# Eight Strassen-like pairs of the second product beside the last column tiles of gate and up

## The chip, the cores and the metric

The kernel runs on one core of a Trainium2 chip. Engines: TensorE (PE, with its weight load PEld), VectorE (DVE), ScalarE (ACT), GpSimd (POOL) and SyncE (SP, here only the queue that issues transfers). PSUM, which PE writes, is used as eight banks of one tile each (128 partitions x 512 float32). Times are device microseconds; the metric is the median of several runs.

## The reference, cut to what matters

```
# DEPTH = 2, SEQ = 256, D_MODEL = 1024, D_FF = 2816
def swiglu(x, w_in, w_out):
    h = x @ w_in
    gate, up = h[..., :D_FF], h[..., D_FF:]
    return (jax.nn.silu(gate) * up) @ w_out
...
for l in range(DEPTH):
    x = layer_norm(ALPHA * x + 0.5 * swiglu(x, ffn1_w_in[l], ffn1_w_out[l]), ln_g[l, 0], ln_b[l, 0])
    mix = hybrid_mixer(x, ...)        # two kinds of attention, one input and one output projection
    x = layer_norm(ALPHA * x + mix, ln_g[l, 1], ln_b[l, 1])
    x = layer_norm(ALPHA * x + 0.5 * swiglu(x, ffn2_w_in[l], ffn2_w_out[l]), ln_g[l, 2], ln_b[l, 2])
```

Four feed-forwards run, named here by layer and place: 00, 02, 10 and 12 (the last). The change is in them alone; the mixer stays as it is.

## The kernel before

All float32 products are made of parts: a value is split into a high part (`wh`, a cast on ACT) and the rest (`wl`, a subtraction on DVE), and three matmuls (high x high, high x rest, rest x high) take the place of one. Weights come through the class `Weights`: a transfer on SP into one of five `raw` buffers of 128 x 1024, then `wh` on ACT and `wl` on DVE, each into one of nine buffers. `get(i)` has the next weights prepared as far as `LOOK` + 1 = 9 slots go. These splits have lower priority (`high_priority(-LATER)`) in the order that a scheduler makes for DVE, ACT and SP. On PE the order is that of the code (`manual_schedule`).

A feed-forward has four stages:

- `first`: the first four column tiles of gate and up as one product of 1024 columns.
- 18 column tiles j = 4 to 21 by `col`, mostly in pairs. Each has a gate half `hg` and an up half `hu`; a half is 8 matmuls of 512 columns (`wide`, both token tiles with high and rest of x) and 8 of 256 columns (`narrow`), in one PSUM bank. Two tiles use four banks, and the next two the other four. The *gather* of a half is an ACT copy of the bank's second part and a DVE add (`L434`, `L435`); after it the bank is free. Then ACT makes silu, DVE the product, and `g` is split for the second product.
- The second product, `w_out`: 22 row tiles of 128 rows. A row tile k is either ordinary (`step`: 12 matmuls of 512 columns for both token tiles t) or half of a pair q (rows 2q, 2q+1) that is multiplied by a Strassen-like scheme (`pair`): 7 products of 3 matmuls, 21 in place of 24, on sums of g (`sums`, four DVE operations, a cast and a subtraction) and on sums of weights (`_make_pair`: two transfers `raw..a`, `raw..b`, a third raw buffer `raw..t` for sums, four DVE sums, and splits named `b`, `t`, `a` of 1024 and `f` of 512 columns). Before, `STR` names six pairs, and `PLAN` sets them among three ordinary tiles, after all column tiles. Accumulators are four banks `acc` (token tile, half of the columns) and four `pp` (products 5, 7, 1, 6).
- The tail: `TAIL` = 7 ordinary row tiles for token tile 0, the layer norm of token tile 0, the same row tiles for token tile 1, and between them (`TCUT` = 3 steps before the end) the transposes `tr_y` of the normalized tile 0.

What waits for what is set by semaphores: a matmul that starts a new tile in a bank waits for the last reader of the old one, a transfer into a raw buffer for its last reader, a split for its transfer.

Of the kernel before, what the change touches and what calls it, by code (L numbers as in the profile page):

```python
# [33 lines left out]
TAIL = 7  # L34
SPLIT = 3
TCUT = 3
LOOK = 8
# [3 lines left out]
STR = (3, 4, 5, 6, 7, 8)  # L41
PLAN = "o o S o S S S S S"
# [17 lines left out]
class Weights:  # L60
# [6 lines left out]
    def _halves(self, i, raw, nm=""):  # L67
        nc = self.nc
        n = raw.shape[-1]
        wh = self.pool.tile([P, 1024], F32R, tag="wh", name=f"wh{i}{nm}", bufs=9)  # L70
        wl = self.pool.tile([P, 1024], F32R, tag="wl", name=f"wl{i}{nm}", bufs=9)
        nc.scalar.copy(wh[:, 0:n], raw)
        nc.vector.tensor_tensor(wl[:, 0:n], raw, wh[:, 0:n].bitcast(F32), ALU.subtract)
        return [tuple(w[:, c : c + 512] for w in (wh, wl)) for c in range(0, n, 512)]
# [21 lines left out]
    def _slots(self, i):  # L96
        return 4 if self.srcs[i][0] == "S" else 1

    def _make(self, i):
# [4 lines left out]
        wh = self.pool.tile([P, 1024], F32R, tag="wh", name=f"wh{i}", bufs=9)  # L104
        wl = self.pool.tile([P, 1024], F32R, tag="wl", name=f"wl{i}", bufs=9)
# [30 lines left out]
def encoder_kernel(  # L136
# [36 lines left out]

    singles = [k for k in range(JT) if k // 2 not in STR]
    singles, tail = singles[: len(singles) - TAIL], singles[len(singles) - TAIL :]
    plan, left, pairs = [], list(singles), list(STR)
    for u in PLAN.split():
        plan.append((u, (left if u == "o" else pairs).pop(0)))
    assert not left and not pairs

    def out_rows(w):
        row = lambda k: w[k * P : (k + 1) * P, :]
        rows = [row(k) if u == "o" else ("S", row(2 * k), row(2 * k + 1)) for u, k in plan]
        return rows + [row(k) for k in tail]

    srcs = []
    for l in range(DEPTH):
        srcs += [f1_b[l, k] for k in range(KT)]
        srcs += [f1_in[l, j, s] for j in range(JT - NB) for s in range(2)]
        srcs += out_rows(f1_out[l])  # L190
# [8 lines left out]
        srcs += [f2_b[l, k] for k in range(KT)]  # L199
        srcs += [f2_in[l, j, s] for j in range(JT - NB) for s in range(2)]  # L200
        srcs += out_rows(f2_out[l])
# [159 lines left out]
    def ffn(l, n, last=False):  # L361
        nonlocal wi
        nm = f"{l}{n}"
        gs = [gp.tile([P, 2, 2, SEQ], F32R, tag="g", name=f"g_{nm}_{q}") for q in range(JT // 2)]
# [29 lines left out]
        def first_t(gv, t):  # L394
# [3 lines left out]
            for q in range(2):  # L398
                a = slice(t * P, (t + 1) * P)
                dh = gs[q][:, :, 0, a]  # L400
                nc.scalar.copy(dh, tr[:, 2 * q : 2 * q + 2, :])
                dv.tensor_tensor(gs[q][:, :, 1, a], tr[:, 2 * q : 2 * q + 2, :], dh.bitcast(F32), ALU.subtract)

        def col(*js, flip=False):
# [3 lines left out]
            for j in js:  # L408

                hs = [ps.tile([P, 2, SEQ], F32, tag="b", name=f"h{'gu'[s]}_{nm}_{j}") for s in range(2)]  # L410
                tl = tp.tile([P, 2, SEQ], F32, tag="tl", name=f"tl_{nm}_{j}", bufs=2)
                ws = [W.get(wi), W.get(wi + 1)]
                wi += 2
                ts.append((j, hs, tl, ws))

            def wide(hs, ws, s):
                for k in range(KT):

                    mm(hs[s], ws[s][0][:, k * P : (k + 1) * P], xx[:, k], start=(k == 0 and not flip),  # L419
                       stop=(k == KT - 1 and flip), skip_group_check=flip)  # L420

            def narrow(hs, ws, s):
                for k in range(KT):
                    mm(hs[s][:, 1, :], ws[s][1][:, k * P : (k + 1) * P], xx[:, k, 0], start=(k == 0 and flip),  # L424
                       stop=(k == KT - 1 and not flip), skip_group_check=flip)

            one, two = (narrow, wide) if flip else (wide, narrow)
            for j, hs, tl, ws in ts:
                for s in range(2):
                    one(hs, ws, s)  # L430
            for j, hs, tl, ws in ts:
                for s in range(2):
                    two(hs, ws, s)
                    nc.scalar.copy(tl[:, s], hs[s][:, 1, :])  # L434
                    dv.tensor_tensor(tl[:, s], hs[s][:, 0, :], tl[:, s], ALU.add)  # L435
                nc.scalar.activation(tl[:, 0], tl[:, 0], AF.Silu)  # L436
                gv = tl[:, 1]
                dv.tensor_tensor(gv, tl[:, 0], gv, ALU.mult)  # L438
                q, jj = divmod(j, 2)
                n = P if q in STR and jj == 0 else SEQ  # L440
                nc.scalar.copy(gs[q][:, jj, 0, 0:n], gv[:, 0:n])  # L441
                dv.tensor_tensor(gs[q][:, jj, 1, 0:n], gv[:, 0:n], gs[q][:, jj, 0, 0:n].bitcast(F32), ALU.subtract)
                if q in STR and jj:
                    sums(q, ts[0][2][:, 1], gv)

        sm = {}

        def sums(q, g0, g1):

            f = tp.tile([P, 4, P], F32, tag="tmp", name=f"sf_{nm}_{q}")  # L450
            if STR.index(q) < 3:
                s = xp.tile([P, 2, 4, P], F32R, tag="x", name=f"s_{nm}_{q}")
                sh, sl = s[:, 0], s[:, 1]
            else:
                sh, sl = (tp.tile([P, 4, P], F32R, tag="tmp", name=f"s{c}_{nm}_{q}") for c in "hl")
# [22 lines left out]
        for j in (NB + 1, *range(NB + 2, JT, 2)):  # L478

            col(*((j,) if j == NB + 1 else (j, j + 1)), flip=(j % 4 == 0 or j == NB + 1))  # L480
# [3 lines left out]
            if j == JT - 6:  # L484
                gb = load_gb(l, n)
                if n == 0:
                    load_mix(l)

        k0, k1 = singles[0], tail[-1]
        kl = tail[-SPLIT]  # L490
        acc = [[(slice(512 * h, 512 * h + 512), ps.tile([P, 512], F32, tag="b", name=f"acc_{nm}_{t}{h}"),
                 k0, tail[-SPLIT - 1] if last and t and h else k1) for h in range(2)] for t in range(2)]
# [12 lines left out]
        pp = {}  # L505

        def pair(q, w, first, final):
            b11, b21, b22, t4, t1, t2, t3 = w
            if first:
                for c in (5, 7, 1, 6):  # L510
                    pp[c] = ps.tile([P, 512], F32, tag="b", name=f"pp_{nm}_{c}")
            sh, sl = sm[q]
            blk = lambda kk, t: [gs[q][:, kk, e, t * P : (t + 1) * P] for e in range(2)]
            smb = lambda c: (sh[:, c], sl[:, c])
            s1, s2, s3, s4 = (smb(c) for c in range(4))
            for o, (ah, al), (bh, bl) in (
                (acc[0][0][1], blk(1, 0), b21),
                (acc[0][1][1], s4, b22),
                (pp[5], s1, t1),
                (pp[7], s3, t3),  # L520
                (pp[1], blk(0, 0), b11),
                (pp[6], s2, t2),
                (acc[1][0][1], blk(1, 1), t4),
            ):
                own = any(o is p for p in pp.values())
                for e, (g, ww) in enumerate(((ah, bh), (ah, bl), (al, bh))):
                    mm(o, g, ww, start=(own and first and e == 0), stop=(own and final and e == 2))  # L527

        for u, k in plan:
            w = W.get(wi)  # L530
            wi += 1
            if u == "S":
                pair(k, w, k == STR[0], k == STR[-1])
# [448 lines left out]
```

## Time and profile before

| | |
|---|---|
| median of three runs | 930.16 us (928.87 to 930.35) |
| the profiled execution: own time, span | 929.28 us, 927.5 us |
| mean granted TensorE clock | 0.997 |
| busy: PE, DVE, ACT | 919.1 us (99%), 804.9 us (87%), 577.8 us (62%) |
| `wl` splits on DVE (L119) | 325.2 us in 271 |
| `wh` casts on ACT (L118) | 282.1 us in 271 |
| transfer of 512 KB, issue to landing | 4.4 to 4.5 us (median) |
| chain that ended last | PE 98% |

A row of a profile's timeline gives start, length, engine, line, operation, the tile written and those read, shapes and count, and in brackets the idle time of the engine before it and what ended it. Lengths overlap: an engine starts its next instruction before the last one has ended. The interval from start to start is what an instruction costs in a row of them.

### The profile page before, as it was taken

What the parts mean: (1) busy time and instruction counts of PE and PEld (TensorE: products, weight loads), DVE (VectorE), ACT (ScalarE), POOL (GpSimd) and SP (SyncE); (2) the same over time, 40 slices, a digit from 0 to 9 for tenths busy, and PEclk for the clock granted to TensorE, in tenths of its full rate; (3) what the DMA queues carried; (4) which work ended last, traced back from release to release, by engine and by line L of the source; (5) the groups of instructions that cost most, each with busy time, mean ns of one, the idle gap of its engine ahead of it and who ended that gap; (6) DMA issues with size and microseconds to landing.
All of it is one profiled execution on the core that took longest, in us unless ns stands there. A gap on an engine that the chain in (4) does not pass through costs nothing.

```text
span 927.5 us, 13795 instructions
## 1 busy us (share of the span) xinstructions
PE 919.1 (99%) x4958; PEld 784.9 (85%) x4958; DVE 804.9 (87%) x1388; ACT 577.8 (62%) x982; POOL 17.0 (2%) x27
## 2 busy tenths in 40 slices
PE   9999999999999999999999999999999999999996
PEld 6888888888878888888888888888888888888885
DVE  7898899998987677899986888999988876888997
ACT  5768656546865666656646666664478656666660
POOL 0000000000000000000000000000000000000000
PEclk9999999999999999999999999999999999999998
DMA  8976445774426755545775665466844365665451
GB/s 320 313 265 203 160 137 191 246 260 154 128 90 206 248 182 182 159 136 191 257 262 196 187 192 168 136 231 208 290 112 137 100 236 188 189 192 163 136 205 46
DMA packets 51380, 176.30 MB, mean 190 GB/s; under 512 B 6512, under 2 KB 8304, under 8 KB 51312
## 3 DMA queue, kind: packets, MB, share of 16 engines
q1 hardware_dynamic: 51024, 175.03, 58.0%
q8 instruction: 39, 0.64, 0.3%
q10 hardware_dynamic: 288, 0.39, 0.1%
q14 instruction: 29, 0.24, 0.1%
HBM read 174.35 MB, written 1.05 MB: 189 GB/s over the span
## 4 chain that ended last, share of the span: by engine, by line
PE 98%; DMA 1%; DVE 1%; SPq 0%; issue 0%; ACT 0%; DVEq 0%
PE hg L419 14%; PE hu L419 14%; PE acc L503 12%; PE hb L381 9%; PE hu L424 7%; PE hg L424 7%; PE pp L527 7%; PE acc L527 5%; PE ao L840 5%; PE os L776 1%; PE pj_sq L617 1%; PE pj_sq L619 1%; PE pj_dv L617 1%; PE pj_sq L618 1%; PE pj_dq L618 1%; PE pj_dv L619 1%
## 5 line engine op out<-in xcount | busy, mean ns | idle before, releaser
L119 DVE TENSOR_TENSOR wl<-raw,wh 128x1024 fp32r<-128x1024 f32 (+1 forms) x271 | 325.2, 1207 | 57.0 <-PE hg L424 20.2
L118 ACT CAST wh<-raw 128x1024 fp32r<-128x1024 f32 (+1 forms) x271 | 282.1, 1046 | 99.7 <-PE acc L503 14.8
L419 PE MATMUL hg<-xx,wh 128*128 128x512 f32 x576 | 143.1, 390 | 0.0
L419 PE MATMUL hu<-xx,wh 128*128 128x512 f32 x576 | 142.3, 389 | 0.0
L419 PEld LDWEIGHTS hu<-xx,wh 128*128 128x128 f32 x576 | 108.1, 188 | 22.5
L419 PEld LDWEIGHTS hg<-xx,wh 128*128 128x128 f32 x576 | 106.6, 188 | 21.2
L503 PE MATMUL acc<-wh,g 128*128 128x512 f32 (+1 forms) x326 | 90.5, 386 | 0.0
L424 PE MATMUL hg<-xx,wl 128*128 128x256 f32 x576 | 81.0, 283 | 0.0
L424 PE MATMUL hu<-xx,wl 128*128 128x256 f32 x576 | 80.9, 283 | 0.0
L424 PEld LDWEIGHTS hg<-xx,wl 128*128 128x128 f32 x576 | 75.4, 191 | 1.6
L424 PEld LDWEIGHTS hu<-xx,wl 128*128 128x128 f32 x576 | 74.3, 192 | 0.0
L503 PEld LDWEIGHTS acc<-wh,g 128*128 128x128 f32 x326 | 60.9, 188 | 12.2
L381 PE MATMUL hb<-wh,xx 128*128 128x512 f32 x256 | 69.5, 391 | 0.4 <-ACT wh L118 0.4
L381 PEld LDWEIGHTS hb<-wh,xx 128*128 128x128 f32 x256 | 47.7, 188 | 11.3 <-ACT wh L118 1.6
L503 PE MATMUL acc<-wl,g 128*128 128x512 f32 (+1 forms) x163 | 51.7, 385 | 0.0
L434 ACT COPY tl<-hg 128x256 f32<-128x256 f32 x72 | 26.7, 371 | 30.9 <-PE hg L419 27.4
L434 ACT COPY tl<-hu 128x256 f32<-128x256 f32 x72 | 26.9, 373 | 19.6 <-PE hu L424 16.8
L381 PE MATMUL hb<-wl,xx 128*128 128x512 f32 x128 | 38.9, 390 | 0.0
L441 ACT CAST g<-tl 128x128 fp32r<-128x128 f32 (+1 forms) x72 | 26.7, 371 | 19.2 <-DVE tl L438 18.2
L840 PE MATMUL ao<-wh,xx 128*128 128x512 f32 x128 | 37.0, 398 | 0.0
L503 PEld LDWEIGHTS acc<-wl,g 128*128 128x128 f32 x163 | 30.6, 188 | 6.1
L436 ACT ACTIVATE tl<-tl 128x256 f32<-128x256 f32 x72 | 30.1, 418 | 6.5 <-DVE tl L435 5.7
(1140 smaller groups left out, 1576.3 us busy)
## 6 DMA issues: line engine op xcount, KB each, us to landing
raw<-in_f_in_dram SPq DMA_DIRECT2D x144, 512.0 KB, 4.4
raw<-in_f_out_dram SPq DMA_DIRECT2D x40, 512.0 KB, 4.5
raw<-in_m_in_dram SPq DMA_DIRECT2D x36, 512.0 KB, 4.4
raw<-in_f_b_dram SPq DMA_DIRECT2D x29, 512.0 KB, 4.3
raw<-in_m_out_dram SPq DMA_DIRECT2D x8, 512.0 KB, 5.0
raw<-in_m_out_dram SPq DMA_DIRECT2D x16, 256.0 KB, 4.4
lng<-in_ln_g_dram SPq DMA_DIRECT2D x6, 512.0 KB, 4.9
lnb<-in_ln_b_dram SPq DMA_DIRECT2D x6, 512.0 KB, 6.2
```

The lines of the kernel that those rows point to most:

```text
L118: nc.scalar.copy(wh[:, s], raw[:, s])
L119: nc.vector.tensor_tensor(wl[:, s], raw[:, s], wh[:, s].bitcast(F32), ALU.subtract)
L381: mm(hb[s], xx[:, k, g, t, :], ww[:, 512 * s : 512 * s + 512], start=(k == 0 and e == 0), stop=(k == KT - 1 and e == 2))
L419: mm(hs[s], ws[s][0][:, k * P : (k + 1) * P], xx[:, k], start=(k == 0 and not flip), stop=(k == KT - 1 and flip), skip_group_check=flip)
L424: mm(hs[s][:, 1, :], ws[s][1][:, k * P : (k + 1) * P], xx[:, k, 0], start=(k == 0 and flip), stop=(k == KT - 1 and not flip), skip_group_c ...
L434: nc.scalar.copy(tl[:, s], hs[s][:, 1, :])
L436: nc.scalar.activation(tl[:, 0], tl[:, 0], AF.Silu)
L441: nc.scalar.copy(gs[q][:, jj, 0, 0:n], gv[:, 0:n])
L503: mm(a, g, ww[:, s], start=(k == ka and e == 0), stop=(k == kb and e == 2))
L527: mm(o, g, ww, start=(own and first and e == 0), stop=(own and final and e == 2))
L617: mm(o, xx[:, k, 0, t, :], wh[:, s], start=(k == 0), stop=False)
L840: mm(acc[t][h], xx[:, k, g, t, :], ww[:, s], start=(k == 0 and e == 0), stop=(k == KT - 1 and e == 2))
```

## The change

`STR` has eight pairs (row tiles 4 to 19), and the tail six ordinary tiles (0 to 3, 20, 21). The stage of the second product between column tiles and tail is gone: beside each column tile j = 14 to 21 runs one pair, j - 14. `pair` is a generator now: three products (9 matmuls), then the gate half of tile j, four products (12 matmuls), then the up half. All seven products have an accumulator bank of their own through this stage, so gate half and up half share the one bank that is left. Three of the seven serve as `acc` in the tail; the fourth `acc`, c22, gets its bank after the stage. The weights' buffers go from nine to eight (`LOOK` = 7), a pair counts three slots instead of four, and the 512-column split `f` gets two buffers of its own. The sums of the later pairs lie in the pool of `g`.

```
-TAIL = 7
+TAIL = 6
...
-LOOK = 8
+LOOK = 7
...
-STR = (3, 4, 5, 6, 7, 8)
-PLAN = "o o S o S S S S S"
+STR = (2, 3, 4, 5, 6, 7, 8, 9)
+MIX = 14
...
+        tag, bufs = ("", LOOK + 1) if n == 1024 else ("f", 2)
+        wh = self.pool.tile([P, n], F32R, tag="wh" + tag, name=f"wh{i}{nm}", bufs=bufs)
...
     def _slots(self, i):
-        return 4 if self.srcs[i][0] == "S" else 1
+        return 3 if self.srcs[i][0] == "S" else 1
...
+        def gather(h, tl, s):
+            nc.scalar.copy(tl[:, s], h[:, 1, :])
+            dv.tensor_tensor(tl[:, s], h[:, 0, :], tl[:, s], ALU.add)
...
+        def half(j, s, tl):
+            nonlocal wi
+            h, w = bank(j, s), W.get(wi)
+            wi += 1
+            wide(h, w)
+            narrow(h, w)
+            gather(h, tl, s)
...
-            if STR.index(q) < 3:
-                s = xp.tile([P, 2, 4, P], F32R, tag="x", name=f"s_{nm}_{q}")
-                sh, sl = s[:, 0], s[:, 1]
-            else:
-                sh, sl = (tp.tile([P, 4, P], F32R, tag="tmp", name=f"s{c}_{nm}_{q}") for c in "hl")
+            pool, tag = (xp, "x") if STR.index(q) < 3 else (gp, "g")
+            s = pool.tile([P, 2, 4, P], F32R, tag=tag, name=f"s_{nm}_{q}")
...
+            todo = ((2, blk(1, 0), b21), (3, s4, b22), (5, s1, t1), (7, s3, t3),
+                    (1, blk(0, 0), b11), (6, s2, t2), (4, blk(1, 1), t4))
+            for m, (c, (ah, al), (bh, bl)) in enumerate(todo):
+                if c not in pp:
+                    pp[c] = ps.tile([P, 512], F32, tag="b", name=f"pp_{nm}_{c}")
+                if m == 3:
+                    yield
+                for e, (g, ww) in enumerate(((ah, bh), (ah, bl), (al, bh))):
+                    mm(pp[c], g, ww, start=(i == 0 and e == 0), stop=(c in (1, 5, 6, 7) and i == len(STR) - 1 and e == 2))
+            yield
+
+        for j in range(MIX, JT):
+            tl = tl_tile(j)
+            if j - MIX < len(STR):
+                w = W.get(wi)
+                wi += 1
+                run = pair(j - MIX, w)
+            for s in range(2):
+                if j - MIX < len(STR):
+                    next(run)
+                half(j, s, tl)
+            gated(j, tl)
+            loads(j)
...
+        c22 = ps.tile([P, 512], F32, tag="b", name=f"acc_{nm}_11")
+        acc = [[(lo, pp[2], None, tail[-1]), (hi, pp[3], None, tail[-1])],
+               [(lo, pp[4], None, tail[-1]), (hi, c22, tail[0], tail[-SPLIT - 1] if last else tail[-1])]]
```

In the rows below a name has its stage (02 is the second feed-forward of layer 0) and tile in it. On PE the end of the column tiles and the start of the second product stood so before:

```order
L424 MATMUL hg_02_21_4278<-xx_78,wl128_4048 128x256 x8
L424 MATMUL hu_02_21_4279<-xx_78,wl129_4054 128x256 x8
L419 MATMUL hg_02_20_4249<-xx_78,wh126_4032 128x512 x8
L419 MATMUL hu_02_20_4250<-xx_78,wh127_4038 128x512 x8
L419 MATMUL hg_02_21_4278<-xx_78,wh128_4047 128x512 x8
L419 MATMUL hu_02_21_4279<-xx_78,wh129_4053 128x512 x8
L503 MATMUL acc_02_00_4367<-wh130_4155,g_02_0_3127 128x512
```

Now PE runs, at tile 18 of the same feed-forward, from the end of the pair's first three products through the gate half into the fourth:

```order
L531 MATMUL pp_02_5_3972<-wl124t_4280,s_02_6_3930 128x512
L531 MATMUL pp_02_5_3972<-wh124t_4279,s_02_6_3930 128x512
L409 MATMUL hg_02_18_4410<-xx_78,wh125_4302 128x512 x8
L414 MATMUL hg_02_18_4410<-xx_78,wl125_4303 128x256 x8
L531 MATMUL pp_02_7_3976<-wh124t_4279,s_02_6_3930 128x512
L531 MATMUL pp_02_7_3976<-wl124t_4280,s_02_6_3930 128x512
```

The halves no longer follow each other in four banks: 12 matmuls of the pair, of which these show the first two, stand between `hg` and `hu` of a tile, and 9 between `hu` and the next `hg`.

On DVE, between the gathers of tiles 20 and 21, there stood before (`hu_02_20` to `hg_02_21`):

```order
L435 TENSOR_TENSOR tl_02_20_4251<-hu_02_20_4250,tl_02_20_4251 128x256
L438 TENSOR_TENSOR tl_02_20_4251<-tl_02_20_4251 128x256
L119 TENSOR_TENSOR wl133_4283<-raw133_4281,wh133_4282 128x1024
L442 TENSOR_TENSOR g_02_10_3137<-tl_02_20_4251,g_02_10_3137 128x256
L435 TENSOR_TENSOR tl_02_21_4280<-hg_02_21_4278,tl_02_21_4280 128x256
```

Now there stand, right behind the gather of `hu_02_17` and up to that of `hg_02_18`, these:

```order
L89 TENSOR_TENSOR raw127a_4375<-raw127b_4376,raw127t_4377 128x512
L424 TENSOR_TENSOR tl_02_17_4264<-tl_02_17_4264 128x256
L74 TENSOR_TENSOR wl127b_4386<-raw127b_4376,wh127b_4385 128x1024
L476 TENSOR_TENSOR sf_02_8_4366<-tl_02_16_4157,tl_02_17_4264 128x128
L430 TENSOR_TENSOR g_02_8_4257<-tl_02_17_4264,g_02_8_4257 128x256
L477 TENSOR_TENSOR sf_02_8_4366<-tl_02_16_4157,sf_02_8_4366 128x128
L90 TENSOR_TENSOR t4_127_4380<-raw127b_4376,raw127a_4375 128x512
L479 TENSOR_TENSOR sf_02_8_4366<-tl_02_17_4264,sf_02_8_4366 128x128
L74 TENSOR_TENSOR wl127t_4390<-raw127t_4377,wh127t_4389 128x1024
L74 TENSOR_TENSOR wl127a_4394<-raw127a_4375,wh127a_4393 128x1024
L481 TENSOR_TENSOR s_02_8_4367<-sf_02_8_4366,s_02_8_4367 128x512
L419 TENSOR_TENSOR tl_02_18_4374<-hg_02_18_4410,tl_02_18_4374 128x256
```

The preparation of the next pair (127) and the sums of tiles 16 and 17 moved in between the two gathers.

In the tail of the first feed-forward the layer norm of token tile 0 ended so on DVE before:

```order
L352 SCALAR_TENSOR_TENSOR x_000_1906<-x_000_1906,mv_000_1912,lng00_1237 128x512 x2
L355 SCALAR_TENSOR_TENSOR x_000_1906<-x_000_1906,rs_000_1914,lnb00_1239 128x512 x2
L119 TENSOR_TENSOR wl63_1848<-raw63_1846,wh63_1847 128x1024
L343 SCALAR_TENSOR_TENSOR x_001_1977<-acc_00_10_1465,x_in1_603 128x512
L332 TENSOR_TENSOR xx_78<-tr_y0000_1954,xx_78 128x4x128
```

and ends so now:

```order
L350 SCALAR_TENSOR_TENSOR x_000_1941<-x_000_1941,mv_000_1947,lng00_1315 128x512 x2
L353 SCALAR_TENSOR_TENSOR x_000_1941<-x_000_1941,rs_000_1949,lnb00_1317 128x512
L341 SCALAR_TENSOR_TENSOR x_001_2006<-pp_00_4_1074,x_in1_598 128x512
L353 SCALAR_TENSOR_TENSOR x_000_1941<-x_000_1941,rs_000_1949,lnb00_1317 128x512
L342 BN_STATS st_001_2007<-x_001_2006 128x6
```

The first add of token tile 1 (`x_001`, from the accumulator `pp_00_4`) moved ahead of the last step of tile 0.

152 lines of the change are left out of this document (69 added, 83 removed).

## The prediction

> **What bounds the kernel now.** I read the page first, then TensorE's waits, the chain of waits, and the busy time by stage.
>
> ```profile
> span 927.5 us, 13795 instructions
> ...
> PE 919.1 (99%) x4958; PEld 784.9 (85%) x4958; DVE 804.9 (87%) x1388; ACT 577.8 (62%) x982; POOL 17.0 (2%) x27
> ```
>
> TensorE (PE) is busy 99% of the span. All its recorded waits are two, 1.2 us together:
>
> ```profile
> PE wps L217 <- PEq L971: 0.8, 1, 0.8
> PE hb L381 <- ACT wh L118: 0.4, 1, 0.4
> ```
>
> So a removed matmul is worth its interval, and a new wait on PE costs its whole length. The intervals come from the chain of waits, here of the layer-0 second feed-forward (start, length, what):
>
> ```profile
> 375.06 0.96 PE hg L424 x8
> ...
> 406.46 5.44 PE acc L503 x24
> ...
> 443.18 17.00 PE acc L503 x75
> 460.18 0.87 PE tr_y L327 x8
> ```
>
> A matmul of 512 columns takes 5.44/24 = 17.00/75 = 0.2267 us, a narrow one of 256 columns 0.96/8 = 0.12.
>
> The busy time by stage shows who could become the next bound. Columns: window, length, then PE, PEld, DVE, ACT, POOL busy, granted clock, DMA share, GB/s. The first two stages are column tiles, the third is the second product, the fourth its tail.
>
> ```profile
> 306.05:354.77 48.72, 48.72 (x293) 43.64 (x293) 35.67 (x68) 30.59 (x55) 0.00 (x0) 1.00 0.61 193
> 354.77:406.46 51.69, 51.69 (x289) 45.38 (x289) 44.64 (x82) 33.97 (x61) 0.00 (x0) 1.00 0.53 164
> 406.46:443.18 36.72, 36.72 (x164) 30.41 (x163) 35.46 (x43) 22.88 (x27) 0.00 (x0) 1.00 0.57 188
> 443.18:463.14 19.96, 19.96 (x94) 16.60 (x93) 19.96 (x30) 11.91 (x13) 0.92 (x1) 1.00 0.71 244
> ```
>
> VectorE (DVE) is busy 35.46 of 36.72 us while pairs are made, and PE has no gap: nothing on PE waits there for DVE within a few microseconds, because weights are prepared eight buffers ahead. The clock is full, so it enters no term.
>
> **The change, part by part.**
>
> *Matmuls.* A feed-forward's second product has 10 ordinary row tiles of 12 matmuls and 6 pairs of 21: 246. Afterwards 6 x 12 + 8 x 21 = 240. Four feed-forwards: 24 x 0.2267 = **-5.44 us**, all on PE, all on the path. The matmuls of the columns are the same, in another order.
>
> *DVE work of the mixed stage.* The preparation of one pair, in DVE's timeline of the second product:
>
> ```profile
> 146.97 0.69 DVE L86 TENSOR_TENSOR raw51t<-raw51a 128x512 f32<-128x512 f32 x1
> 147.57 0.69 DVE L87 TENSOR_TENSOR raw51t<-raw51a,raw51b 128x512 f32<-128x512 f32 x1
> 148.18 1.22 DVE L73 TENSOR_TENSOR wl51b<-raw51b,wh51b 128x1024 fp32r<-128x1024 f32 x1
> 149.31 0.68 DVE L88 TENSOR_TENSOR raw51a<-raw51b,raw51t 128x512 f32<-128x512 f32 x1
> ...
> 153.39 0.68 DVE L86 TENSOR_TENSOR raw52t<-raw52a 128x512 f32<-128x512 f32 x1
> ```
>
> From start to start a 512-column operation takes 0.60 and a 1024-column one 1.135; a pair is 153.39 - 146.97 = 6.42 us, against 21 x 0.2267 = 4.76 of PE. A column tile on PE is 16 x 0.2267 + 16 x 0.12 = 5.55. So a mixed tile is 10.31 us of PE. DVE's part of a column tile needs rows of the timelines around one column, PE, ScalarE (ACT) and DVE:
>
> ```profile
> 102.25 1.98 PE L419 MATMUL hg<-xx,wh 128*128 128x512 f32 x8
> ...
> 104.31 0.37 ACT L434 COPY tl<-hg 128x256 f32<-128x256 f32 x1 [0.34 <-PE hg L419]
> 104.58 1.05 ACT L118 CAST wh<-raw 128x1024 fp32r<-128x1024 f32 x1
> ...
> 105.15 0.42 DVE L438 TENSOR_TENSOR tl<-tl 128x256 f32<-128x256 f32 x1
> 105.48 0.42 DVE L435 TENSOR_TENSOR tl<-hg,tl 128x256 f32<-128x256 f32 x1
> 105.82 0.28 DVE L459 TENSOR_TENSOR sf<-tl 128x128 f32<-128x128 f32 x1
> 106.02 0.28 DVE L442 TENSOR_TENSOR g<-tl,g 128x128 fp32r<-128x128 f32 x1
> ```
>
> 256 columns take 0.335, 128 take 0.20. Two neighbouring mixed tiles: two pairs 12.84, four weight splits 4.54, four gathers 1.34, two products 0.67, splits of g 0.535, sums 4 x 0.20 + 0.60 = 1.40: 21.3 us of DVE against 20.62 of PE. DVE becomes as loaded as PE, with no reserve.
>
> *One bank for both halves.* Seven products hold seven banks, so the gate half and the up half of a tile take turns in the eighth. The next half's first matmul now waits until the gather (ACT copy, DVE add) of the half before has read it; behind it on PE stands everything. Hiding it are the pair matmuls between: 12 (2.72 us) after a gate half, 9 (2.04) after an up half. Call L the time from a half's last result to the start of its DVE add. The rows show the earliest case (result 104.23, copy from 104.31 for 0.37): L is at least 0.5; the actual add started at 105.48, L = 1.25. The next half can issue 2.72 - 0.16 after the result (a narrow matmul's result comes 0.28 after its issue in the trace, its interval is 0.12); the add takes 0.42. So PE stalls once L exceeds 2.56 - 0.42 - 0.05 = 2.09 after a gate half, and 1.41 after an up half.
>
> L follows from DVE's order, which the listing in the part on the change shows. Between the up gather of tile 17 and the gate gather of tile 18 in the second feed-forward stand: gather 0.335, 0.60, 0.335, split 1.135, 0.20, 0.335, 0.20, 0.60, 0.20, two splits 2.27, 0.60: 6.81 us. PE needs only 4.82 there (9 matmuls and one half, 2.04 + 2.78). So L grows by 1.99 in that step. By the same addition the steps ahead of it give L = 0.5 at the up half of 16, then +0.32 and +0.04 in the two steps: 0.86 at the up half of 17, then 2.85. The stall is 2.85 - 2.09 = 0.76 us, and the same pattern comes back at tile 20. How much PE loses more in a restart no row shows; between 0 and 0.16 (result time over interval), I take 0.1. The feed-forwards with the number 02, 10 and 12 have the same DVE order, so 6 x 0.86 = 5.2 us if DVE never waits itself.
>
> *DVE waits itself.* In ACT's order the copy of every up half stands behind the cast of the next pair's second row tile, and this tile's transfer waits for a raw buffer that the `wl..t` split of the pair before frees. The price of that ring:
>
> ```profile
> 139.17 1.22 DVE L73 TENSOR_TENSOR wl49a<-raw49a,wh49a 128x1024 fp32r<-128x1024 f32 x1
> ```
> ```profile
> 140.42 0.33 SPq L82 DMA_DIRECT2D raw51b<-in_f_out_dram  x1
> ```
> ```profile
> raw51b<-in_f_out_dram SPq DMA_DIRECT2D x1, 512.0 KB, 4.3
> raw52a<-in_f_out_dram SPq DMA_DIRECT2D x1, 512.0 KB, 3.5
> raw52b<-in_f_out_dram SPq DMA_DIRECT2D x1, 512.0 KB, 4.9
> ```
>
> Split 1.22, issue 0.03 after its end (140.39 to 140.42), landing 4.3, cast 0.95 to 1.05, copy 0.37 and a little: about 6.95 us from the split's start to the gather. DVE's own work in between adds up to 6.68. So each up gather comes some 0.27 later than by DVE's work alone; with the slowest landing (4.9) 0.9, with a quick one (3.5) nothing. Taking 0.27, L before the first lump is 1.13 and the stall 3.12 - 2.09 = 1.03. A stall sets L back: at the up half of 18 it is 2.09 - 1.69 + 0.27 = 0.67 (that step has 3.81 of DVE for 5.50 of PE), then 0.99, 1.30 and 3.29, a second stall of 1.20. With two restarts that is 2.43 us in each of three feed-forwards: 7.3. In the first feed-forward the order has no such lump (its longest step, 6.07 against 5.50, brings L to 1.39, against 1.41): between 0 and 1.6, I take 0.8. Together **+8.1 us**; bounds 2.4 and 14 (both worked out with the rivals).
>
> *Eight weight buffers for nine.* The mixer and the first column tiles are prepared one buffer less ahead. PE has no wait there now, and DVE's slack of 48.72 - 35.67 = 13 us in the first column stage covers it. I take 0, with 1.5 as the upper bound (an estimate: four second products that end with buffers full, one wait as long as the 0.4 that PE shows at the start for each).
>
> *The tail.* After the last matmul of the first token tile PE has 33 matmuls (7.48 us) before the transposes, afterwards 27 (6.12). The layer norm in that time must be done. In the first feed-forward DVE's order now puts the first add of the second token tile, which waits for PE's ninth-last matmul, ahead of the layer norm's last step of the first one. Transposes there now:
>
> ```profile
> 181.97 0.66 PE tr_y L327 x4
> ...
> 183.29 1.84 PE acc L503 x8
> ```
>
> 1.32 against 0.87 elsewhere (460.18), so 0.45 is lost already. Afterwards the second four transposes wait for the result (0.2), two DVE operations of 512 columns (0.6 each, 0.1 for their ends); the first four's 0.44 counts against it: 1.1 lost, **+0.7 us** more; bounds 0 and 1.5. In the other feed-forwards the order is as before and 6.12 us just covers it: 0, at most 0.6 each.
>
> *Sum.* -5.44 + 8.1 + 0.7 = +3.4 on the profiled execution's 929.28: 932.6. The median of the runs (930.16) lies 0.88 above that execution, so the forecast is **933.5 us**, +0.36%. What the measurement can tell from no change is about 0.2%, 1.9 us: 928.3 to 932.0 counts as the same.
>
> One rule speaks against the shared bank. The Trainium skill, page "Perfetto Trace Analysis", section "Matmuls", says that independent matmul groups should rotate through different PSUM banks, so that the evacuation of one overlaps the next group's matmuls. The trace of before rotates, and has no wait there. By that rule alone the second bank would be worth the whole 8.1 us, and without the shared bank the sum would be -4.7; the pair's matmuls between the halves replace the rotation only up to the lags above.
>
> **The rivals.**
>
> *Faster: the lag stays at its floor.* If each up gather starts at 0.5 (transfers land in 3.5, DVE's small operations run a little closer), the first lump gives 2.49 and a stall of 0.40, no restart: 6 x 0.40 = 2.4, nothing in the first feed-forward. -5.44 + 2.4 + 0.7 = -2.3: 927.8 by the median; with the lumps hidden altogether, 925.4. For it: 13 us of DVE slack before the stage, and in the second product DVE is busy 97% without a gap on PE. Against it: the order of DVE is fixed, and 6.81 us do not go into 4.82. It decides below L = 0.5 at the up half of 17. Chance 0.22.
>
> *No change: DVE is the only limit.* Transfers are early enough, the lumps cost 0.86: -5.44 + 5.2 + 0.4 + 0.7 = +0.9, by the median 931.0. For it: two of the three landings above, 4.3 and 3.5, leave DVE's wait at 0.3 or nothing. Against it: the third, 4.9. Chance 0.28.
>
> *Much slower: both transfers of a pair wait for the same split.* Where the first row tile takes the buffer of `wl..t` and the second stands behind it in SyncE's queue, the second lands about 0.9 later; then DVE idles 0.9 at every second up half, L passes 1.41 there too, and each feed-forward loses 3.5: -5.44 + 14 + 0.7, by the median 939.4. Against it: the buffers change places from pair to pair. Chance 0.13.
>
> *Starved mixer.* If the eighth buffer is what keeps the mixer's first matmuls fed: +1.5 over the forecast, 935. Chance 0.04.
>
> **How the numbers follow.** My forecast 0.33, the others as above. Faster 0.22; same 0.28, slower 0.33 + 0.13 + 0.04 = 0.50. The range goes from 926.5 (inside the faster rival, which reaches to 925.4) to 939; the likeliest case's own range is 931.5 to 936.
>
> **What would show it.** Right: TensorE waiting for `tl` (the gather's add), longest before the up halves of tiles 18 and 20 in three feed-forwards, 0.7 to 1.3 us each; DVE busy over 95% from tile 14 on; ACT waiting for a transfer ahead of the up copies; transposes in the first feed-forward taking 2 us for 1.3; mixer without waits. Wrong: stalls spread over all halves (the transfer ring, or ACT's order, is the bound and not the lumps), PE waiting for `wl` (weights late), or no stall at all and 5 us gained.

## The result, and the profile after

The changed kernel takes 943.42 us (median of four runs, 942.86 to 944.39) against 929.88 us (928.87 to 930.35) before: 1.0148 times as long, 95% interval 1.0131 to 1.0166. The forecast was 933.5 us with a range from 926.5 to 939. The direction was right, the size was not. The profiled execution took 944.39 us, its mean granted clock was 0.998.

The page of after, its span and busy times:

```profile
span 942.6 us, 13784 instructions
...
PE 922.7 (98%) x4934; PEld 778.7 (83%) x4934; DVE 843.0 (89%) x1476; ACT 577.8 (61%) x1003; POOL 17.0 (2%) x27
```

The span is 15.1 us longer with 24 matmuls fewer. DVE has 38.1 us more to do than before (843.0 against 804.9), and its instructions went from 1388 to 1476. TensorE's waits (what waits, what ended the wait; us in total, times, longest) say whom PE now waits for:

```profile
PE hu L409 <- DVE tl L419: 6.1, 6, 1.0
PE pj_dk L644 <- DVE wl L120: 2.2, 3, 1.0
PE hg L409 <- DVE tl L419: 1.2, 3, 0.6
PE pp L562 <- DVE wl L120: 0.9, 1, 0.9
PE tr_y L325 <- DVE x L353: 0.9, 2, 0.7
...
PE pj_dk L645 <- DVE xx L330: 0.2, 1, 0.2
```

The first row is the forecast stall: six times ahead of an up half, each about 1 us. They stand at tiles 18 and 20 of the feed-forwards 02, 10 and 12, and nowhere else. Of the three waits in the third row the two long ones (0.65 and 0.34) are the first feed-forward's; the third (0.18) stands in 02. The rows with `wl` are waits for weights, at the end of the first feed-forward (`pp`) and at the start of the mixers (`pj_dk`, its first projection), which the forecast put at zero. The last row is a wait for the mixer's own input `xx`.

A window of 02 from the up half of tile 14 to the first matmuls of the tail (columns as in the prediction) shows DVE busy 82.96 of 85.70 us, 97%:

```profile
375.90:461.60 85.70, 83.50 (x420) 70.02 (x420) 82.96 (x125) 52.68 (x80) 0.00 (x0) 1.00 0.66 213
```

The first lump of 02, from the timelines of SP, ACT, DVE and PE, and the transfer's row (KB, us from issue to landing):

```profile
404.44 0.33 SPq L83 DMA_DIRECT2D raw127a<-in_f_out_dram  x1
404.48 1.22 DVE L74 TENSOR_TENSOR wl124t<-raw124t,wh124t 128x1024 fp32r<-128x1024 f32 x1
405.77 0.33 SPq L83 DMA_DIRECT2D raw127b<-in_f_out_dram  x1
...
409.25 1.12 PE L414 MATMUL hu<-xx,wl 128*128 128x256 f32 x8
410.55 1.05 ACT L73 CAST wh127b<-raw127b 128x1024 fp32r<-128x1024 f32 x1 [3.83 <-DMA raw127b<-in_f_out_dram]
411.50 0.36 ACT L418 COPY tl<-hu 128x256 f32<-128x256 f32 x1
411.90 0.43 DVE L419 TENSOR_TENSOR tl<-hu,tl 128x256 f32<-128x256 f32 x1 [0.66 <-ACT tl L418]
412.38 2.11 PE L409 MATMUL hg<-xx,wh 128*128 128x512 f32 x8
414.33 1.11 PE L414 MATMUL hg<-xx,wl 128*128 128x256 f32 x8
...
418.12 0.68 DVE L481 TENSOR_TENSOR s<-sf,s 128x512 fp32r<-128x512 f32 x1
418.73 0.41 DVE L419 TENSOR_TENSOR tl<-hg,tl 128x256 f32<-128x256 f32 x1
419.20 2.12 PE L409 MATMUL hu<-xx,wh 128*128 128x512 f32 x8 [1.01 <-DVE tl L419]
```
```profile
raw127b<-in_f_out_dram SPq DMA_DIRECT2D x1, 512.0 KB, 4.7
```

Read it in order. The second row tile of pair 127 waits for a raw buffer: it is issued at 405.77, right behind the end of the split `wl124t` of the pair before (404.48 + 1.22 = 405.70) and 1.33 us behind the first row tile, and lands 4.7 us later; ACT stood idle 3.83 us for it, so its cast, the copy of `hu` behind the cast and DVE's add (0.66 idle) are all late. The lag L after the up half of 17 is 411.90 - 410.37 (end of its last narrow matmul) = 1.53 us; 1.13 was forecast. DVE's long order between the two gathers then makes it 418.73 - 415.44 = 3.29 after the gate half of 18; 3.12 was forecast. The up half starts 1.17 us late, against a forecast of 1.03 and 1.20 for the two lumps.

The waits that were not forecast, and the transposes, from PE's timeline:

```profile
176.29 0.74 PE L562 MATMUL pp<-wl,g 128*128 128x512 f32 x2 [0.88 <-DVE wl L120]
...
185.54 0.66 PE L325 MATMUL tr_y<-ident,x 128*128 128x128 f32 x4 [0.15 <-DVE x L353]
186.92 0.63 PE L325 MATMUL tr_y<-ident,x 128*128 128x128 f32 x4 [0.73 <-DVE x L353]
193.54 0.50 PE L644 MATMUL pj_dk<-wl,xx 128*128 128x512 f32 x1 [0.96 <-DVE wl L120]
```

A matmul starts later than the shown wait says: the row at 419.20 shows 1.01 and starts 1.17 late, the one at 193.54 shows 0.96 and starts 1.13 late. By late starts (start to start, less the usual interval) the waits sum to 15.07 us, against 0.33 before:

| where | late starts, us | forecast |
|---|---|---|
| six lumps, tiles 18 and 20 of 02, 10, 12 | 7.02 | 6.7 |
| 00: gate halves of tiles 15 and 19 | 1.31 | 0.8 |
| 00: transposes | 1.19 (0.33 before) | +0.7 |
| 00: last matmuls, waiting for `wl` | 1.27 | 0 |
| mixers: first projections, waiting for `wl` (0.32 of it for `xx`) | 3.36 | 0 |
| other places of 02, 10, 12 | 0.94 | 0 |

The rest is slow running: -5.44 + 15.07 - 0.33 = 9.3, the span grew by 15.1, so 5.8 us lie in intervals that are each a little longer. Compared place by place some 5.2 of them are found: after a late start the eight wide matmuls take some 2.12 us (1.98 before, `102.25` in the prediction), whether it is 1.17 us late (row at 419.20) or only 0.10 with no wait shown (row at 412.38), and the nine and twelve pair matmuls behind a narrow group take 2.07 and 2.75 us, where 0.2267 each would be 2.04 and 2.72.

### The profile page after: what moved, and what is told of

It is laid out like the page before. It is cut to its first block, busy times and chain, and to the rows that moved or that the text cites. A ratio compares the mean times of both kernels' runs of the same rounds, so it can differ in the third digit from the quotient of the medians.

```text
span 942.6 us, 13784 instructions
## 1 busy us (share of the span) xinstructions
PE 922.7 (98%) x4934; PEld 778.7 (83%) x4934; DVE 843.0 (89%) x1476; ACT 577.8 (61%) x1003; POOL 17.0 (2%) x27
## 5 line engine op out<-in xcount | busy, mean ns | idle before, releaser
L120 DVE TENSOR_TENSOR wl<-raw,wh 128x1024 fp32r<-128x1024 f32 (+1 forms) x255 | 304.7, 1205 | 28.3 <-ACT wh L119 12.7
L119 ACT CAST wh<-raw 128x1024 fp32r<-128x1024 f32 (+1 forms) x255 | 264.2, 1045 | 101.9 <-PE acc L562 21.2
L382 PEld LDWEIGHTS hb<-wh,xx 128*128 128x128 f32 x256 | 48.2, 190 | 10.9 <-ACT wh L119 1.0
L562 PE MATMUL pp<-wh,g 128*128 128x512 f32 x144 | 43.2, 390 | 0.0
L419 DVE TENSOR_TENSOR tl<-hu,tl 128x256 f32<-128x256 f32 x72 | 30.1, 417 | 7.4 <-ACT tl L418 7.2
L419 DVE TENSOR_TENSOR tl<-hg,tl 128x256 f32<-128x256 f32 x72 | 30.0, 417 | 4.0 <-ACT tl L418 3.9
L480 ACT CAST s<-sf 128x512 fp32r<-128x512 f32 x32 | 19.8, 618 | 21.3 <-DVE sf L479 21.3
```

The source lines that it names most:

```text
L119: nc.scalar.copy(wh[:, s], raw[:, s])
L120: nc.vector.tensor_tensor(wl[:, s], raw[:, s], wh[:, s].bitcast(F32), ALU.subtract)
L382: mm(hb[s], xx[:, k, g, t, :], ww[:, 512 * s : 512 * s + 512], start=(k == 0 and e == 0), stop=(k == KT - 1 and e == 2))
L419: dv.tensor_tensor(tl[:, s], h[:, 0, :], tl[:, s], ALU.add)
L480: nc.scalar.copy(sh, f)
L562: mm(a, g, ww[:, s], start=(k == ka and e == 0), stop=(k == kb and e == 2))
```

## The experiments

Each kernel ran with the kernel before beside it on the same chip; a ratio is to that. The first is an edit of the kernel before, the others are edits of the kernel after, or of an edit named.

**Eight weight buffers alone, without the rest of the change** (kernel before).

```
-LOOK = 8
+LOOK = 7
...
-        wh = self.pool.tile([P, 1024], F32R, tag="wh", name=f"wh{i}", bufs=9)
-        wl = self.pool.tile([P, 1024], F32R, tag="wl", name=f"wl{i}", bufs=9)
+        wh = self.pool.tile([P, 1024], F32R, tag="wh", name=f"wh{i}", bufs=LOOK + 1)
+        wl = self.pool.tile([P, 1024], F32R, tag="wl", name=f"wl{i}", bufs=LOOK + 1)
```

> The kernel before, with eight weight buffers in place of nine (LOOK 7) and nothing else. Theory A, the missing buffer is what the mixers pay for in the changed kernel: PE waits for wl at pj_dk in both mixers, about 2.7 us in layer 0 and 1.4 in layer 1, so the time is 3 to 4.5 us above before (933 to 934.5). Rival B, the mixers' waits come from DVE being late at the end of the changed feed-forward: no such wait here, and less than 1 us of difference.

Measured: 937.91 us, 1.0087 (1.0072 to 1.0102), +8.2 us. The mixers' waits come, as theory A said, but the time is about twice what it gave. The TensorE waits for DVE:

```profile
PE pj_dk L618 <- DVE wl L119: 4.0, 4, 1.3
PE acc L503 <- DVE wl L119: 1.8, 4, 0.7
```

DVE's and PE's timelines at the start of the first mixer:

```profile
186.41 1.22 DVE L119 TENSOR_TENSOR wl<-raw,wh 128x1024 fp32r<-128x1024 f32 x1
187.54 0.69 DVE L344 BATCH_NORM_STATS2 st<-x 128x6 f32<-128x512 f32 x1
188.14 1.21 DVE L119 TENSOR_TENSOR wl<-raw,wh 128x1024 fp32r<-128x1024 f32 x1
189.26 0.20 DVE L346 BATCH_NORM_AGGREGATE mv<-st 128x2 f32<-128x12 f32 x1
189.40 0.50 PE L618 MATMUL pj_dk<-wl,xx 128*128 128x512 f32 x1 [1.31 <-DVE wl L119]
```

PE waits 1.31 us for the split that started at 188.14. It stands among layer-norm steps of token tile 1 (L344, L346): where a feed-forward ends, DVE has the norm to do besides the splits, while PE takes the next weights without a pause. In the kernel before DVE does the same in the same order (this split starts at 188.36 there), and PE has no wait. So the ninth buffer is the reserve there. The mixers wait where the changed kernel's do, and each is 2.6 us longer up to the end of the next `first` stage (123.2 against 120.6). The waits in the tail lie elsewhere: in 02, 10 and 12 here, in 00 in the changed kernel. So one buffer costs the old kernel 8.2 us, more than the changed kernel's own waits for `wl`.

**The up half's bank.** Product 4 is added into product 7's bank, so that gate half and up half have a bank each again; the two products' separate sums are left out.

```
-                    pp[c] = ps.tile([P, 512], F32, tag="b", name=f"pp_{nm}_{c}")
+                    pp[c] = pp[7] if c == 4 else ps.tile([P, 512], F32, tag="b", name=f"pp_{nm}_{c}")
...
-        c22 = ps.tile([P, 512], F32, tag="b", name=f"acc_{nm}_11")
+        c21, c22 = (ps.tile([P, 512], F32, tag="b", name=f"acc_{nm}_1{h}") for h in range(2))
```

> The changed kernel, but product 4 of every pair is added into the bank of product 7, so that gate and up halves have two banks to take turns in; the accumulator of token tile 1 starts afresh in the tail. It leaves out the separate sum of product 4; all instructions of the mixed stage stay. Theory A, the shared bank turns DVE's lags into stalls: the waits of hg and hu for tl (7.3 us), their restarts and slow starts vanish, some 9 to 11 us: 932 to 934.5. Rival B, DVE (21.3 us of work for 20.6 of PE per two tiles) is the bound and the stalls come back as PE waiting for wl: less than half of that is gained, above 938.

Measured: 939.64 us, 1.0096 (1.0074 to 1.0118): 3.8 us less than the changed kernel. The profiled execution, at 935.58, was quicker than the other three (939.55 to 939.91), so its waits do not show where those lost 4 us more:

```profile
PE tr_y L325 <- DVE x L353: 3.6, 4, 2.0
PE pj_dk L644 <- DVE wl L120: 2.5, 4, 1.0
PE pp L562 <- DVE wl L120: 1.2, 1, 1.2
```

No wait for `tl` is left; the waits at the transposes grew from 0.9 to 3.6 us instead (2.19 us late in 02, 0.87 in 10). DVE was behind, and where the bank no longer held PE up, PE met DVE at the next place where they meet, the layer norm. The gain is as small as rival B said, but what waits is mostly the transposes and not the weights. So the shared bank is where PE waited, but taking it away gives back only part of the 7.3 us of waits for `tl`; that DVE's load is the cause of the rest is argued here, not shown.

**DVE's order.** The gather gets priority over everything else.

```
         def gather(h, tl, s):
-            nc.scalar.copy(tl[:, s], h[:, 1, :])
-            dv.tensor_tensor(tl[:, s], h[:, 0, :], tl[:, s], ALU.add)
+            with tc.high_priority():
+                nc.scalar.copy(tl[:, s], h[:, 1, :])
+                dv.tensor_tensor(tl[:, s], h[:, 0, :], tl[:, s], ALU.add)
```

> The changed kernel with the gather (the ACT copy and DVE add of a half) at high priority for the scheduler, and nothing else; the shared bank stays. In the order that results the steps of 6.81 us of DVE between the up gather of tile 17 (19) and the gate gather of 18 (20) are gone; the longest excess of DVE over PE between two gathers is 0.85 in place of 1.99. Theory A, the uneven order is the cause of the stalls at tiles 18 and 20: the six of 1.17 us vanish with their restarts, 7 to 9 us, 934.5 to 936.5. Rival B, the ring of raw buffers delays each up gather by 0.3 to 0.7, and as DVE has no reserve the lags add up and the stalls come back elsewhere: less than 3 us gained, above 940.5.

Measured: 939.51 us, 1.0103 (1.0076 to 1.013), 3.9 less than the changed kernel. Its two largest waits:

```profile
PE hg L409 <- DVE tl L420: 3.4, 7, 0.8
PE pj_dk L645 <- DVE wl L120: 2.3, 3, 1.0
```

The six waits ahead of up halves are gone, so they were a matter of DVE's order, as forecast. Ahead of gate halves there are now seven (at most 0.8) where there were three. The gain lies between the two theories: the long stalls vanish as A said, and part of them comes back elsewhere as B said.

**Nine buffers, with and without that order.** Nine weight buffers again; the room comes from the pool of `g` (11 buffers to 9).

```
-LOOK = 7
+LOOK = 8
...
-    gp = ctx.enter_context(tc.tile_pool(name="gp", bufs=11))
+    gp = ctx.enter_context(tc.tile_pool(name="gp", bufs=9))
```

With the gather first as well:

> As the one with the gather at high priority, and with nine weight buffers again (LOOK 8); the room comes from the pool of g, 9 tiles in place of 11, whose waits do not change the order. If the mixers' waits are due to the buffers, theirs (4.1 us) and the tail's wait for wl in the first feed-forward (1 us) go too: 929 to 932, about the kernel before. If not: 934 to 937, as with the priority alone.

Measured: 932.55 us, 1.0025 (1.0014 to 1.0036), 0.6 above the range for the buffers as cause and clear of the other. Its waits, the lines with `tl` and the transposes:

```profile
PE tr_y L325 <- DVE x L353: 1.4, 1, 1.4
PE hu L409 <- DVE tl L420: 1.0, 3, 0.5
PE hg L409 <- DVE tl L420: 0.8, 2, 0.5
```

Without it:

> The changed kernel with nine weight buffers again (LOOK 8, g pool of 9) and no priority for the gather. The order of DVE comes out without the long steps of 1.99 at tiles 18 and 20 by itself; its longest excess between two gathers is 1.66 in the first feed-forward and 1.05 in the others. Theory A, the buffer is worth the mixers' waits (4.1 us), the tail's wl (1.3) and, by the order that it brings, most of the lumps (7): 931 to 934, as with both edits. Rival B, the order by priority did most of it: 936 or more.

Measured: 939.96 us, 1.0112 (1.0093 to 1.013). Its waits:

```profile
PE hu L409 <- DVE tl L419: 3.9, 4, 2.3
PE hg L409 <- DVE tl L419: 3.0, 5, 1.5
PE tr_y L325 <- DVE x L353: 1.3, 1, 1.3
...
PE pj_dk L644 <- DVE wl L120: 0.7, 1, 0.7
```

The wait of the mixers for `wl` falls from 2.2 to 0.7 us (to nothing with both edits), and the one in the tail of 00 is gone: most of these waits are the missing buffer's. But alone the ninth buffer brings 3.5 us only, since the waits for `tl` stay and move (6.9 us, the longest 2.3). My expectation that it would bring most was wrong.

**Six `raw` buffers.** Added to the kernel with both edits (pool of `g` 8), then alone on the changed kernel (pool of `g` 10).

```
-        r0, r1, ta = (self.pool.tile([P, 1024], F32, tag="raw", name=f"raw{i}{c}", bufs=5) for c in "abt")
+        r0, r1, ta = (self.pool.tile([P, 1024], F32, tag="raw", name=f"raw{i}{c}", bufs=6) for c in "abt")
...
-        raw = self.pool.tile([P, 1024], F32, tag="raw", name=f"raw{i}", bufs=5)
+        raw = self.pool.tile([P, 1024], F32, tag="raw", name=f"raw{i}", bufs=6)
```

> Gather first, nine weight buffers, and six raw buffers for five (g pool of 8). The order of DVE stays nearly as it was. Theory A, the ring of raw buffers delays the up gathers (the transfer of the next pair's second tile waits for the split of the pair before): DVE's waits ahead of the up gathers vanish, and with them the stalls of 0.4 to 0.6 at tiles 14 to 17: 1 to 3 us less than with five (932.6), 929.5 to 931.5. Rival B, DVE's work alone sets the lag: within 0.7 us of it.

Measured: 929.47 us, 0.9994 (0.9985 to 1.0003), 3.1 less than with five and as fast as the kernel before. Of PE's waits for DVE one line is left, and none for `tl`:

```profile
PE pj_dk L645 <- DVE wl L120: 2.0, 2, 1.4
```

Both are in the mixer of layer 0. In layer 1 PE waits for `wl` in none of the three kernels with nine buffers. In layer 0 it waits in each of them, at the transposes of 00, here, or at both, so what is left there is not the missing buffer's.

> The changed kernel with six raw buffers in place of five (g pool of 10) and nothing else. The order of DVE up to tile 18 stays in the feed-forwards 02, 10 and 12, with the step that is 1.99 too long. Theory A, transfers that wait for a raw buffer added 0.6 to the lag ahead of that step: DVE no longer waits before the up gather of tile 17, the lag there is 0.9 for 1.54, and the stall at 18 is 0.6 to 0.9 for 1.17; with the other stalls 3 to 5 us gained, 938.5 to 940.5; the mixers' waits stay. Rival B, the order alone makes the stall: 1.17 stays, less than 1.5 us gained.

Measured: 936.14 us, 1.0064 (1.0051 to 1.0077), 7.3 less than the changed kernel. Its waits for `tl`, and the first lump of 02 as above:

```profile
PE hu L409 <- DVE tl L419: 1.5, 3, 0.5
PE hg L409 <- DVE tl L419: 0.9, 3, 0.4
```
```profile
401.97 0.33 SPq L83 DMA_DIRECT2D raw127b<-in_f_out_dram  x1
...
405.15 1.05 ACT L73 CAST wh127b<-raw127b 128x1024 fp32r<-128x1024 f32 x1 [0.90 <-DMA raw127b<-in_f_out_dram]
...
407.94 0.37 ACT L418 COPY tl<-hu 128x256 f32<-128x256 f32 x1 [1.73 <-PE hu L414]
...
415.99 1.20 PE L409 MATMUL hu<-xx,wh 128*128 128x512 f32 x4 [0.51 <-DVE tl L419]
```

The transfer is issued 5.0 us behind the one before (396.98) instead of 1.33 and lands 3.1 us after its issue, long before the half is done; the copy waits for PE alone. DVE's order up to the gather at tile 18 is the same as in the changed kernel, and the start at tile 18 is 0.67 late instead of 1.17. So at tile 18 about 0.5 of the lump came from the ring of raw buffers, and 0.67 from DVE's order. The gain is more than the expected 3 to 5: the waits ahead of the up halves of tile 20 and those of the first feed-forward for `tl` are gone too, the former with another order of DVE.

The three edits, alone and together:

| gather first | weight buffers | `raw` | median, us | against after |
|---|---|---|---|---|
| no | 8 | 5 | 943.42 | |
| yes | 8 | 5 | 939.51 | -3.9 |
| no | 9 | 5 | 939.96 | -3.5 |
| no | 8 | 6 | 936.14 | -7.3 |
| yes | 9 | 5 | 932.55 | -10.9 |
| yes | 9 | 6 | 929.47 | -14.0 |

The single gains add up to 14.7, near the 14.0 of all three. Between them they do not simply add: the first two bring 7.4 apart and 10.9 together, and the sixth `raw` buffer 7.3 alone and 3.1 behind them. Six `raw` buffers with just one of the other two edits were not run.

**The sums of g on GpSimd.** The four `sf` subtractions of a pair go from DVE to GpSimd, in the last kernel of that table.

```
-            dv.tensor_tensor(f[:, 0], a21, a22, ALU.subtract)
+            nc.gpsimd.tensor_tensor(f[:, 0], a21, a22, ALU.subtract)
...
-            dv.tensor_tensor(f[:, 3], a12, f[:, 1], ALU.subtract)
+            nc.gpsimd.tensor_tensor(f[:, 3], a12, f[:, 1], ALU.subtract)
```

> As the one with six raw buffers, and the four small subtractions of each pair's sums on GpSimd, which is idle, in place of DVE; that takes 0.8 us of DVE from two tiles, 20.5 for 20.6 of PE. Theory A, DVE is the bound of the mixed stage: the remaining stalls there get shorter, 1 to 2 us less, and the time is below before: 927.5 to 929.5. Rival B, GpSimd is slow at it, or in DVE's way: the sums come late, PE waits for s, and the time rises by more than 1 us.

Measured: 960.56 us, 1.0332 (1.0317 to 1.0347). One of its four groups on GpSimd and DVE's split of the sums, by line (busy us, mean ns of one, idle time before them), then a stretch of both timelines:

```profile
L477 POOL TENSOR_TENSOR sf<-tl,tl 128x128 f32<-128x128 f32 x32 | 53.3, 1664 | 127.0 <-DVE tl L425 127.0
L482 DVE TENSOR_TENSOR s<-sf,s 128x512 fp32r<-128x512 f32 x32 | 22.1, 691 | 37.1 <-ACT s L481 37.1
```
```profile
397.31 3.45 POOL L477 TENSOR_TENSOR sf<-tl,tl 128x128 f32<-128x128 f32 x1 [6.77 <-DVE tl L425]
...
399.76 0.68 DVE L87 TENSOR_TENSOR raw124t<-raw124a 128x512 f32<-128x512 f32 x1
400.84 0.46 POOL L478 TENSOR_TENSOR sf<-tl,sf 128x128 f32<-128x128 f32 x1
401.74 0.42 DVE L420 TENSOR_TENSOR tl<-hg,tl 128x256 f32<-128x256 f32 x1 [1.30 <-ACT tl L419]
```

On average the subtractions on GpSimd take 0.6 to 1.7 us each where DVE takes 0.28, about 4.6 us for the four. In each of the four groups the quickest takes 0.46, so the averages hang on what DVE does at the time: the one at 397.31 takes 3.45 while DVE runs splits and subtractions without a pause until 400.44 (399.76 + 0.68), and the one at 400.84 takes 0.46 while DVE is idle. DVE's split of the sums (L482) then waits 37.1 us in all, through ACT's cast of them, where it waited 6.5; behind it in DVE's order stand the gathers: PE's waits for `tl` are 25.2 us. DVE itself is slower beside GpSimd as well: the products of L431 take 374 ns where they took 284, and 484 where they took 417 (256 columns). So both halves of rival B are seen, the late sums as the larger, though PE waits for the gathers and not for `s`.

**The first feed-forward's layer norm.** In the changed kernel the norm of token tile 1 loses its priority there, so that the first add no longer stands ahead of tile 0's last step.

```
-        with tc.high_priority():
+        with tc.high_priority(0) if nm == "00" and t else tc.high_priority():
```

> The changed kernel, with the layer norm of token tile 1 in the first feed-forward at normal priority, so that on DVE the last step of token tile 0's norm stands ahead of tile 1's first add; nothing else in the order of DVE changes but this place. Theory A: the wait between the two groups of transposes (0.88 us) vanishes, but since the norm starts late, PE still waits about 0.7 before the first group; 0.5 us gained in the span. Rival B, the whole norm is late and the order does not matter: the wait moves ahead of the transposes, less than 0.2 gained.

One profiled execution: 942.44 us. The waits for weights:

```profile
PE pj_dk L644 <- DVE wl L120: 3.1, 4, 1.6
```

The gap between the two groups of transposes (0.88 late) is gone, so the order that the prediction showed made it. But the mixer's first matmul on `wl` now starts 1.78 us late, where it was 1.13. Both theories expected a longer wait ahead of the transposes in its place; that did not come, and most of the 0.88 went to the mixer. With a single execution the difference in time (1 us) says nothing.

**Both relieved.** The kernel with all three edits of the table, with this norm order and with the mixer's small work on lambda (three DVE operations, an exponential and two more) moved behind the first key transposes.

> The one with gather first, nine weight and six raw buffers, and two edits at the end of the first feed-forward: the layer norm of token tile 1 at normal priority there, and the mixer's small work on lambda (three DVE operations, an exponential on ACT with its table load of 1.28 us, two more DVE operations) later, after the first key transposes. Theory A: the mixer's last waits (2.3 us on wl, layer 0) come from these two standing ahead of two weight splits on DVE and one cast on ACT; they vanish, and the time is 926.5 to 928.5, below the kernel before. Rival B: DVE's total work from the tail to the first rotary step is the bound, as it has some 20 us of it; the wait moves to the transposes or to a later weight, and the time stays within 1 us of 929.5.

Measured: 928.76 us, 0.999 (0.998 to 0.9999). This is inside rival B's 1 us. Its one wait of PE for DVE:

```profile
PE tr_y L325 <- DVE x L353: 2.2, 1, 2.2
```

The mixer's wait (2.0 us) is gone and has come back at the transposes of the first feed-forward, as rival B said. This is the only version of the whole computation whose interval lies below the kernel before, by about 1 us, and only just (0.9999).

**The bank once more,** in that kernel, with the edit of the second experiment (the separate sums left out again).

> The same, with product 4 added into the bank of product 7 and two banks for the halves; it leaves out the separate sum of product 4. Theory A: with an even order and the transfers early, the lags stay under what the pair's matmuls hide, and the shared bank costs nothing any more: within 1 us of the same kernel with one bank. Rival B: each half still pays for the one bank (slow starts behind it): 2 us or more less.

Measured: 927.86 us, 0.9983 (0.9975 to 0.9992): 0.9 us less than the one with a single bank, within theory A's 1 us, and the two intervals overlap. With the lags short, a second bank is worth 1 us at most.

## Why the prediction was wrong

*Matmuls, -5.44.* 24 fewer (4934 against 4958), as said.

*The lumps: right.* Place, number and size held: six at tiles 18 and 20, 7.0 us of late starts where 6.7 were forecast. That the size is so near is in part luck: at tile 18 of 02 the lag ahead of DVE's long step was 1.53 for 1.13, and the step added 1.76 for 1.99, since PE itself started the gate half 0.10 late there and ran its wide matmuls 0.14 slower. Giving the gather priority removes them, which shows the order of DVE as cause; six `raw` buffers, with DVE's order unchanged, cut the one at tile 18 from 1.17 to 0.67, which shows the ring. The ring's share was mis-sized: DVE waits 0.66 us for ACT's copy where 0.27 was taken, because the transfer took 4.7 us, near the slowest of the three rows shown, and not 4.3.

*"Eight weight buffers for nine", 0, at most 1.5: the step that failed.* The cover that it names, 13 us of DVE's slack in the first column stage, is real but lies in the wrong place. The buffers run low where DVE does the layer norm and PE goes on with the mixer. There the changed kernel loses 1.27 + 3.36 = 4.63 us, three times the upper bound; the old kernel with eight buffers loses 8.2 us in all, and nine buffers take most of these waits away. In layer 0 the missing buffer is not the whole cause, since kernels with nine still wait there or at the transposes. The "starved mixer" rival named the mechanism, with a chance of 0.04 and 1.5 us for the 3.4 that the mixers lost. The sign "mixer without waits" failed, and PE waiting for `wl`, a sign of being wrong, came.

*Restarts, 0.1 each: mis-sized, and with 4.6 us as large a part of the miss.* A wait ahead of wide matmuls costs about 0.3 us beyond what is shown (0.16 late, 0.14 slower wide matmuls), and the mixed order itself some 0.06 a tile behind its two narrow groups, about 1.9 us in 32 tiles; this second part was not in the sum. All the small delays found are 5.2 us, where 0.6 was in the sum. What in PE makes them stays open; no run varied the shapes alone.

*The first feed-forward.* Waits for `tl` 1.31 for 0.8, transposes +0.86 for +0.7, by the order named. Its last matmuls' wait for `wl` belongs to the buffers.

*The sum.* Not forecast were 4.6 for the buffers, 4.6 of small delays, 0.9 in other places of 02, 10 and 12, and 1.0 in the stalls that were foreseen: 11.1 of the 11.7 us by which the span's growth (15.1) passed the forecast (3.4). The other 0.6 is not placed.

*The rivals.* "Much slower" gave 939.4 by stalls at every second up half; these didn't come, so its mechanism is out although its time was nearer. "Faster" and "no change" needed lags near the floor; the table shows that it takes three edits to get there. Even then the 5.44 us are not gained: with no wait for `tl`, the feed-forwards 02 and 12 are 0.6 and 0.8 us shorter, not 1.36, 10 is as long as before, and 2 us are lost at the end of 00 or at the mixer's start, wherever DVE's work is put. That DVE's load is what moves the wait from place to place is an inference from three such shifts (the two banks, the norm's order, both relieved); no run took work off DVE without adding waits.

*The rule on banks.* The Trainium skill, page "Perfetto Trace Analysis", section "Matmuls", asks that independent groups rotate through different banks. The second bank was reckoned at the whole 8.1 us; it brought 3.8 in the changed kernel and 0.9 in the kernel with short lags. So here the rule is worth something as far as the reader of the bank is late, and the pair's matmuls between the halves can stand in for the rotation.

## What to carry to other kernels

A buffer fewer is priced where the engine that fills it is busiest with something else, not at the stage with most slack: look for the place where the ring runs empty, here the layer norm and the start of the next block. When a change loads a second engine to 97% beside a full one, a wait that is removed can come back at the next place where the two meet; here the last 2 us moved between transposes and mixer with each edit. So look at where the waits went and not only at the time. Add a price for every new wait beyond its shown length, and for each change of matmul shape.

## What the runs showed of the hardware

- After a wait of about 1 us PE's next matmul started 0.16 us later than the shown wait says, and its first eight wide matmuls took 2.12 us for 1.98. After a start only 0.10 us late, with no wait shown, they took 2.11.
- A transfer of 512 KB landed 4.7 us after its issue when it was issued 1.33 us behind another, and 3.1 us in the kernel with six `raw` buffers, where it was issued 5.0 us behind the one before.
- GpSimd needed 0.46 us at the quickest for a 128 x 128 float32 subtraction, in each of its four groups, and up to 4.2 us in a kernel in which DVE was busy beside it (means 0.60 to 1.68 us); DVE needs 0.28 (rows in the prediction). In the same run DVE's products of 128 columns took 374 ns for 284. Which of DVE's operations hold GpSimd up wasn't tried.
